# A hybrid RG-LRU and short-convolution block on one core: the first tile's root, the sums of squares of chunk 1 and the last sum arranged anew

## Chip, cores and metric

The kernel runs on one core of one Trainium2 chip. The metric is device time in microseconds (us) of one execution; lower is better. Every run is one launch of the whole block on the same inputs.

## What is computed

The block works on 1024 positions of width 1024, all in float32. The part that matters here is the first half of the layer; the last line closes the block.

```python
sc = jax.nn.silu(c)
mod = sc @ ada_w[l] + ada_b[l]
shift1, scale1, gate1, shift2, scale2, gate2 = jnp.split(mod[:, None, :], N_ADA, axis=-1)
h = rmsnorm(x, norm1_g[l]) * (1.0 + scale1) + shift1
proj = h @ w_in[l]                      # 1024 -> 2560
...
x = x + gate1 * mixed
h2 = rmsnorm(x, norm2_g[l]) * (1.0 + scale2) + shift2
x = x + gate2 * (jnp.square(jax.nn.relu(h2 @ w_mlp1[l])) @ w_mlp2[l])
...
return rmsnorm(x, final_g)
```

Between proj and mixed stand a causal convolution, an RG-LRU recurrence, a gated convolution, head-wise norms and an output projection.

## The kernel before

**Layout.** Everything is kept transposed: 128 channels on the partitions, positions along the free axis. The 1024 positions are two chunks of 512 (cc = 0 and 1), the 1024 channels eight tiles (k = 0 to 7). F[:, 8 cc + k] holds tile k of chunk cc. F[:, 16:26], E and G are scratch. A product in high precision is made of three matmuls with rounded operands (`mm3`, L105, L107, L109): each operand is split in a high half (HI, rounded) and a low half (LO, what the rounding left), kept in R; the products are low weights by high data, high by high, and high weights by low data.

**Start (L135 to L310).** SP loads the vectors (`vt`, L141), a unit matrix into G (`ident`, L172) and x of chunk 0 (four DMAs, `load_x`). TensorE spreads silu(c) over all partitions in banks 0 and 1, and VectorE copies them to `cb` (L295). ScalarE squares the eight tiles of x (L292), VectorE adds them up, and float32 matmuls with a matrix of ones (L300) put the sum of squares into bank 7. `rsq` (L119 to L124) makes the reciprocal root: ScalarE's root and its square, then two VectorE instructions that are one step of correction. 21 `warm` matmuls keep TensorE busy meanwhile (L305).

**The loop over the tiles of chunk 0 (L321 to L357).** For tile k+1 VectorE makes two columns of modulation, each with one product with a row sum over 128 x 1024 (`gemv1`, L251), of which ScalarE makes scale and shift (`mod1`, L258 and L260). `make_xn` (L238) multiplies x by the root. `make_hi` is two ScalarE passes: the high half of scale * x + shift into R (L243), and the same unrounded, in place in F (L244). `make_lo` (L247) subtracts the two on VectorE. The weights of the tile are split too: ScalarE rounds them (L327), VectorE makes the remainder (L322). Then TensorE adds the tile to seven banks: 7 blocks of `mm3`, 21 matmuls of 512 columns. The order of the loop body, without the loads:

```python
V.tensor_tensor(whl(k)[1], win1[k], fp(whl(k)[0]), op=ALU.subtract)
if k == 0:
    make_lo(0, k)
if k + 1 < KT:
    gemv1(k + 1, 0)
    A(whl(k + 1)[0], win1[k + 1], AF.Copy)
    make_xn(0, k + 1, r0)
if k:
    make_lo(0, k)
...
    gemv1(k + 1, 1)
    make_hi(0, k + 1)
```

**Sums of chunk 1.** From k = 5 on, ScalarE squares the tiles of chunk 1 (`squares1`, L315), two at a time; VectorE adds each pair and a float32 matmul adds the pair to bank 7 (`sum1`, L318 and L319): one at k = 6, three at k = 7. At k = 7 the matmuls of all banks but the first are ordered behind the last of these sums. Then `softplus2` (small VectorE instructions), `rsq`, and `make_h1` (L361 to L364) and the low half (L371) tile by tile for chunk 1.

**What sets the order.** Up to L371 VectorE, ScalarE and SP work in the order of the program (`manual_schedule`); TensorE's instructions, and everything behind, are ordered by the compiler's scheduler, with `after(a, b)` where an order is written out. ScalarE's copy of a finished bank for the gated convolution (`conv_c`, L470) belongs to what comes behind, and chunk 1's first matmuls (`chunk1`) follow it.

**End (L1043 to L1120).** The last products of the block go in quarters: for half h of chunk cc, `last_acc` adds a block to x, squares it (L1056) and scales it with final_g (L1058); `last_add` adds the square to E[:, cc]; `last_sum` sums E and the square of tile 6 with two float32 matmuls (L1065, L1066); `last_rs` is `rsq`; `last_out` multiplies with the root (L1077 to L1082) and stores (L1083).

Of the kernel before, what the change touches and what calls it, by code (L numbers as in the profile page):

```python
# [14 lines left out]
P = 128  # L15
# [20 lines left out]
def block_kernel(ctx, tc, xT, vec, adaT, winA, winB, gw, wout, w1, w2, outT):  # L36
# [5 lines left out]
    def sb(name, shape, dt=F32):  # L42
        return pool.tile(shape, dt, name=name, tag=name)
# [2 lines left out]
    R = sb("R", [P, 38, 2, H], F32R)  # L46
    F = sb("F", [P, 26, H])
    E = sb("E", [P, 4, 516])
    vt = sb("vt", [P, NV])
    sc = sb("sc", [P, KT])  # L50
    ones = sb("ones", [P, P])
    bones = sb("bones", [P, P], F32R)
# [2 lines left out]
    epsc = sb("epsc", [P, 1])  # L55
    mods = sb("mods", [P, 48])
    md = sb("md", [P, 48])
    pre = sb("pre", [P, 48])
    pg = sb("pg", [P, 8])
    lp = sb("lp", [P, 6, 4])  # L60
    gneg = sb("gneg", [P, 8])
# [10 lines left out]
    def fp(ap):  # L72
        return ap.bitcast(F32)
# [64 lines left out]
    V.memset(bf[:64, :64], 1.0)  # L138
    V.memset(bf[64:, 64:], 1.0)
    V.tensor_copy(bones, bf)  # L140
    dma(vt, vec[:, :NV])  # L141

    def f(i):
        return F[:, i, :]
# [23 lines left out]
        win1[k] = fl(r)[:, : NS * P].rearrange("p (j n) -> p j n", n=P)  # L168
        dma(win1[k], winA[k].rearrange("p (j n) -> p j n", n=P))

    ident = G[:, 0, :P]
    dma(ident, vec[:, NV:])  # L172
    for q in range(4):
        load_x(0, q)

# [86 lines left out]
    def whl(k):  # L262
        w0 = 16 + k // 4
        return R[:, w0 : w0 + 2 * NS : 2, HI, kc(k)], R[:, w0 : w0 + 2 * NS : 2, LO, kc(k)]

    ET = mybir.EngineType
    with tc.manual_schedule(engines={ET.DVE, ET.Activation, ET.SP}):
        V.tensor_scalar(neg, ap, -1.0, None, op0=ALU.mult)
        V.tensor_tensor(neg, neg, ap, op=ALU.min)
        A(e, neg, AF.Exp)  # L270

        cp = vt[:, V_C : V_C + KT]
        A(sc, cp, AF.Tanh, scale=0.5)

        A(lp[:, 5, 0:1], vt[:, 0:1], AF.Abs_reciprocal_sqrt)
        V.scalar_tensor_tensor(sc, sc, 1.0, cp, op0=ALU.add, op1=ALU.mult)
        for k in range(KT):
            i = T.matmul(banks[k // 4][:, kc(k)], lhsT=sc[:, k : k + 1].broadcast_to([P, P]), rhs=ident, start=True, stop=True)
        warm(ones, 8, i)
        V.tensor_scalar(vt[:, V_N1 : V_N1 + 24], vt[:, V_N1 : V_N1 + 24], -1.0 / (2 * D), None, op0=ALU.mult)  # L280
        V.tensor_scalar(gneg, vt[:, V_LOG : V_LOG + 8], -1.0 / 128, None, op0=ALU.mult)
        V.tensor_scalar(pre, vt[:, V_ADAB : V_ADAB + 48], 1.0, None, op0=ALU.add)
        V.tensor_tensor(pg, pre[:, 0:16:2], vt[:, V_N1 : V_N1 + 8], op=ALU.mult)
        softplus1()
        load_ada1(0)
        load_win1(0)
        load_ada1(1)
        load_win1(1)

        sq0 = [f(16), f(17), E[:, 0, :H], E[:, 1, :H], E[:, 2, :H], E[:, 3, :H], f(14), f(15)]  # L290
        for k in range(KT):
            A(sq0[k], f(k), AF.Square)  # L292
            if k % 2:
                if k < 4:
                    V.tensor_copy(cb[:, k // 2, :], banks[k // 2])  # L295
                V.tensor_tensor(sq0[k - 1], sq0[k - 1], sq0[k], op=ALU.add)
            if k == 3:
                V.tensor_tensor(sq0[0], sq0[0], sq0[2], op=ALU.add)
            if k > 2 and k % 2:
                summed = T.matmul(banks[7], lhsT=ones, rhs=sq0[0 if k == 3 else k - 1], start=k == 3, stop=k == 7)  # L300
        r0, r1 = E[:, 0, :H], E[:, 1, :H]
        for i in range(2):
            gemv1(0, i, False)
        rsq(banks[7], r0, r1, D)
        warm(ones, 21, summed)  # L305
        for i in range(2):
            mod1(0, i)
        make_xn(0, 0, r0)
        A(whl(0)[0], win1[0], AF.Copy)
        make_hi(0, 0)  # L310
        sq1 = {6: f(16), 7: f(17), 0: E[:, 1, :H], 1: E[:, 3, :H], 2: E[:, 2, :H], 3: f(17), 4: f(16), 5: E[:, 3, :H]}

        def squares1(k):
            for i in (k, k + 1):
                A(sq1[i], f(8 + i), AF.Square)  # L315

        def sum1(k):
            V.tensor_tensor(sq1[k], sq1[k], sq1[k + 1], op=ALU.add)  # L318
            return T.matmul(banks[7], lhsT=ones, rhs=sq1[k], start=k == 6, stop=k == 4)  # L319

        for k in range(KT):  # L321
            V.tensor_tensor(whl(k)[1], win1[k], fp(whl(k)[0]), op=ALU.subtract)  # L322
            if k == 0:
                make_lo(0, k)
            if k + 1 < KT:
                gemv1(k + 1, 0)
                A(whl(k + 1)[0], win1[k + 1], AF.Copy)  # L327
                make_xn(0, k + 1, r0)
            if k:
                make_lo(0, k)  # L330
            if k + 1 < KT:
                if k == 6:
                    squares1(0)
                gemv1(k + 1, 1)
                make_hi(0, k + 1)
            if k + 2 < KT:
                load_ada1(k + 2)
                load_win1(k + 2)
            if k == 4:
                load_x(1, 3)  # L340
            if k == 5:
                load_x(1, 0)
                load_x(1, 1)
                squares1(6)
            if k == 6:
# [20 lines left out]
        make_h1(0)  # L366
        for k in range(KT):
            if k + 1 < KT:
                hi_done = make_h1(k + 1)
            hi, lo = rs_(2 * k + 1)  # L370
            h_done = V.scalar_tensor_tensor(lo, f(8 + k), md[:, 2 * k + 1 : 2 * k + 2], fp(hi), op0=ALU.add, op1=ALU.subtract)  # L371


    gh, gl = sb("gh", [P, 2 * H], F32R), sb("G", [P, 2 * H], F32R)
# [676 lines left out]
    def last_acc(p, h, q):  # L1051
        cs = cols(h)
        b = ends[h][0 if p == 4 else 1 if p == 2 else 2][q][:, cs]
        cc, n = block2(p, 4 + 2 * q)
        acc2(cc, n, b, cs)
        A(f(14 + n)[:, cs], x1(cc, n)[:, cs], AF.Square)  # L1056
        if n != 6:
            A(x1(cc, n)[:, cs], x1(cc, n)[:, cs], AF.Identity, scale=vt[:, V_NF + n : V_NF + n + 1])  # L1058
# [9 lines left out]
    def last_rs(cc, h):  # L1068
        rsq(nbank[cc, h][:, :Q], E[:, cc, cols(h)], f(24)[:, cols(h)], D)

    def last_out(cc, h, first, step=4):
        cs = cols(h)
        rs = E[:, cc : cc + 1, cs]
        for n in range(0, 4, step) if first else range(4, 8, step):
            o = cc * 8 + n
            if n + step <= 6:
                V.tensor_tensor(F[:, o : o + step, cs], F[:, o : o + step, cs], rs.broadcast_to([P, step, Q]), op=ALU.mult)  # L1077
            else:
                if step == 4:
                    V.tensor_tensor(F[:, o : o + 2, cs], F[:, o : o + 2, cs], rs.broadcast_to([P, 2, Q]), op=ALU.mult)  # L1080
                V.scalar_tensor_tensor(x1(cc, 6)[:, cs], x1(cc, 6)[:, cs], vt[:, V_NF + 6 : V_NF + 7], E[:, cc, cs], op0=ALU.mult, op1=ALU.mult)
                V.tensor_tensor(x1(cc, 7)[:, cs], x1(cc, 7)[:, cs], E[:, cc, cs], op=ALU.mult)  # L1082
            dma(outT[cc, :, n : n + step, cs], F[:, o : o + step, cs])  # L1083
# [88 lines left out]
```

## Time and profile before

| what | value |
|---|---|
| device time, median of 3 runs | 980.53 us (980.26 to 981.69) |
| time of the profiled execution | 980.45 us |
| its span | 978.7 us |
| TensorE matmul (PE) busy | 963.9 us, 98%, 4448 records |
| VectorE (DVE) busy | 750.8 us, 77% |
| ScalarE (ACT) busy | 537.2 us, 55% |
| DMA, q1 | 153.77 MB, 44.8% of 16 engines' span |

The span is what the profiler saw of the core; the execution's time has 1.75 us around it. PE is the matmuls, PEld the loads of their weights, which run beside them. Ends of matmuls are modelled. Start times below count from the start of the span. In a timeline a row has start, duration, engine, line, operation, output <- inputs, sizes and the count of merged instructions; in square brackets stands how long the engine idled before it and what ended that. SPq is SP's queue of DMA issues. Buffer numbers are left out: F, E and R are the tensors named above. A column "granted clock" of 1.00 is 2.4 GHz, 0.50 is 1.2 GHz.

### The profile page before, as it was taken

To read this page: it belongs to the slowest core of one execution; us is meant where nothing else is said; L and a number is where in the kernel's file an instruction comes from. 1 tells how busy PE (TensorE), PEld (TensorE's weight loads), DVE (VectorE), ACT (ScalarE), POOL (GpSimd) and SP (SyncE) were. 2 spreads that over 40 slices of the span, in tenths; PEclk is the share of its full clock that TensorE was granted. 3 is DMA by queue.
4 is the path that set the end of the run, shared out by engine and by line. 5 is a ranking of instruction groups with operands and counts; after the bars stand their busy time and mean duration, and the time that the engine had idled before them with its cause. 6 is when DMAs were issued, how large, how long until landed. Compare 5 with 4: busy or idle time off the path is not lost.

```text
span 978.7 us, 11651 instructions
## 1 busy us (share of the span) xinstructions
PE 963.9 (98%) x4448; PEld 800.2 (82%) x4448; DVE 750.8 (77%) x1001; ACT 537.2 (55%) x719; POOL 0.2 (0%) x4
## 2 busy tenths in 40 slices
PE   8999999999999999999999999999999999999996
PEld 7878787788888998888888888887888888888885
DVE  7989999976545799785655555798598599589757
ACT  6778888885412677555464554683253243144444
POOL 0000000000000000000000000000000000000000
PEclk9999999999999999999999999999999999999998
DMA  8925236234222131774443524789356157144005
GB/s 313 344 100 183 89 138 210 74 125 172 78 95 97 50 115 63 258 255 175 172 145 124 204 104 177 264 286 357 124 173 215 65 172 236 65 151 172 1 1 172
DMA packets 53288, 154.52 MB, mean 158 GB/s; under 512 B 5104, under 2 KB 10736, under 8 KB 53232
## 3 DMA queue, kind: packets, MB, share of 16 engines
q1 hardware_dynamic: 53232, 153.77, 44.8%
q8 instruction: 35, 0.57, 0.2%
q14 instruction: 21, 0.17, 0.0%
HBM read 116.00 MB, written 37.75 MB: 157 GB/s over the span
## 4 chain that ended last, share of the span: by engine, by line
PE 84%; DVE 10%; ACT 3%; DMA 2%; issue 1%; SPq 0%; DVEq 0%; ACTq 0%
PE bank L105 28%; PE bank L109 27%; PE bank L107 27%; DVE R L101 2%; DVE F L212 1%; DVE F L434 1%; DVE F L465 1%; DMA E<-hidd 1%; ACT F L407 1%; DMA gh<-hidd 0%; DMA F<-xT 0%; ACT R L100 0%; DVE F L463 0%; DVE F L466 0%; DMA hidd<-E 0%
## 5 line engine op out<-in xcount | busy, mean ns | idle before, releaser
L105 PE MATMUL bank<-R 128*128 128x512 f32 (+1 forms) x1416 | 522.3, 380 | 1.3 <-ACT R L364 0.6
L107 PE MATMUL bank<-R 128*128 128x512 f32 (+1 forms) x1416 | 519.8, 379 | 0.0
L109 PE MATMUL bank<-R 128*128 128x512 f32 (+1 forms) x1416 | 516.7, 379 | 0.0
L105 PEld LDWEIGHTS bank<-R 128*128 128x128 f32 x1416 | 266.3, 188 | 54.5 <-DVE F L996 1.9
L109 PEld LDWEIGHTS bank<-R 128*128 128x128 f32 x1416 | 266.1, 188 | 50.6 <-DVE R L247 0.4
L107 PEld LDWEIGHTS bank<-R 128*128 128x128 f32 x1416 | 266.4, 188 | 50.3 <-issue 0.7
L100 ACT ACTIVATE R<-F 128x1024 fp32r<-128x1024 f32 (+1 forms) x175 | 165.6, 958 | 175.8 <-PE bank L109 117.6
L101 DVE TENSOR_TENSOR R<-F,R 128x1024 fp32r<-128x1024 f32 (+1 forms) x175 | 189.4, 1098 | 58.0 <-ACT R L100 57.8
L996 DVE SCALAR_TENSOR_TENSOR F<-bank,md,F 128x512 f32<-128x512 f32 (+1 forms) x120 | 84.9, 712 | 49.0 <-PE bank L109 47.7
L909 ACT ACTIVATE F<-bank 128x512 f32<-128x512 f32 x44 | 26.2, 597 | 48.8 <-PE bank L109 48.3
L100 ACT ACTIVATE R<-G 128x1024 fp32r<-128x1024 f32 x23 | 24.3, 1057 | 32.8 <-PE bank L109 22.0
L101 DVE TENSOR_TENSOR R<-G,R 128x1024 fp32r<-128x1024 f32 x23 | 28.1, 1221 | 13.0 <-ACT R L100 13.0
L100 ACT ACTIVATE R<-E 128x1024 fp32r<-128x1024 f32 x26 | 27.4, 1052 | 10.1 <-DMA E<-hidd 10.0
L101 DVE TENSOR_TENSOR R<-E,R 128x1024 fp32r<-128x1024 f32 x26 | 31.7, 1218 | 0.1
L212 DVE SCALAR_TENSOR_TENSOR F<-F 128x1024 f32<-128x1024 f32 x24 | 29.1, 1217 | 1.3 <-DMA F<-adaT 1.3
L585 ACT ACTIVATE E<-F 128x512 f32<-128x512 f32 (+1 forms) x21 | 11.1, 527 | 32.3 <-DVE F L583 30.3
L407 ACT ACT_TABLE_LOAD x22 | 28.2, 1283 | 0.4
L909 ACT ACTIVATE E<-bank 128x512 f32<-128x512 f32 x20 | 11.9, 595 | 23.4 <-PE bank L109 23.4
L583 DVE SCALAR_TENSOR_TENSOR F<-bank,md,F 128x512 f32<-128x512 f32 (+1 forms) x21 | 12.7, 620 | 15.6 <-PE bank L109 15.6
L924 ACT ACTIVATE F<-bank 128x512 f32<-128x512 f32 x16 | 9.5, 597 | 19.9 <-PE bank L109 18.5
L913 ACT ACTIVATE F<-F 128x1024 f32<-128x1024 f32 x18 | 18.9, 1049 | 2.6 <-DVE F L943 1.5
L914 ACT ACTIVATE F<-F 128x1024 f32<-128x1024 f32 x18 | 19.0, 1058 | 0.4
(198 smaller groups left out, 738.2 us busy)
## 6 DMA issues: line engine op xcount, KB each, us to landing
F<-w SPq DMA_DIRECT2D x51, 512.0 KB, 4.2
hidd<-F SPq DMA_DIRECT2D x47, 512.0 KB, 4.5
F<-adaT SPq DMA_DIRECT2D x44, 512.0 KB, 4.1
E<-hidd SPq DMA_DIRECT2D x26, 512.0 KB, 5.7
F<-xT SPq DMA_DIRECT2D x16, 512.0 KB, 5.8
F<-hidd SPq DMA_DIRECT2D x15, 512.0 KB, 4.4
gh<-hidd SPq DMA_DIRECT2D x15, 512.0 KB, 4.9
F<-winB SPq DMA_DIRECT2D x13, 512.0 KB, 3.2
```

What stands on the lines that cost most here:

```text
L100: a = A(dst[0], src, AF.Copy)
L101: return a, V.tensor_tensor(dst[1], src, fp(dst[0]), op=ALU.subtract)
L105: i = [T.matmul(b, lhsT=wl, rhs=xh, start=start, stop=False, **kw) for b, xh, xl in outs]
L107: T.matmul(b, lhsT=wh, rhs=xh, start=False, stop=False, **kw)
L109: T.matmul(b, lhsT=wh, rhs=xl, start=False, stop=stop, **kw)
L212: g = V.scalar_tensor_tensor(fl(r), fl(r), 0.5, fl(cb) if cv is None else cv, op0=ALU.mult, op1=ALU.mult, accum_out=mods[:, idx : idx + 1])
L407: i = A(*args, **kw)
L583: V.scalar_tensor_tensor(x, b, gate(16, n), x, op0=ALU.mult, op1=ALU.add)
L909: A(t[:, q, :], bk2[q], AF.Copy)
L913: A(t, t, AF.Relu)
L914: A(t, t, AF.Square)
L996: done_by["bank"] = V.scalar_tensor_tensor(x1(cc, n)[:, cs], b, gate(40, n), x1(cc, n)[:, cs], op0=ALU.mult, op1=ALU.add)
```

## The change

All vectors and the unit matrix come with one load into a longer `vt`; `ident` and `pre` are views of it, and the +1 is made in place. Of the first eight squares the last is made by VectorE, and the copy of bank 1 by ScalarE. For the first tile of each chunk the correction of the root is no longer finished ahead of the scaling: `first_h` multiplies the tile by column and uncorrected root, then by the corrected factor, and `full_root` finishes the root for the other tiles afterwards. Tiles 0 and 7 of chunk 0 get their low half by `shift_lo`; tiles 1 to 6 get `make_lo` at another place of the loop body. Two squares of chunk 1 are made by VectorE, and its eight squares are summed with three float32 matmuls, all at k = 7. At the end, the last quarter's squares are summed with three matmuls, without the last VectorE add, and the last tiles are scaled in pairs.

```diff
-    vt = sb("vt", [P, NV])
+    vt = sb("vt", [P, NV + P])
-    pre = sb("pre", [P, 48])
-    dma(vt, vec[:, :NV])
+    dma(vt, vec)
-    ident = G[:, 0, :P]
-    dma(ident, vec[:, NV:])
+    ident = vt[:, NV:]
+    pre = vt[:, V_ADAB : V_ADAB + 48]
...
+    def first_h(x, g, r0, r1):
+        V.scalar_tensor_tensor(x, x, g, r0, op0=ALU.mult, op1=ALU.mult)
+        V.scalar_tensor_tensor(r1, banks[7], D * EPS, r1, op0=ALU.add, op1=ALU.mult)
+        V.scalar_tensor_tensor(x, r1, -3.0 * D, x, op0=ALU.add, op1=ALU.mult)
+    def full_root(r0, r1):
+        V.scalar_tensor_tensor(r0, r1, -3.0 * D, r0, op0=ALU.add, op1=ALU.mult)
+    def shift_lo(cc, k):
+        hi, lo = rs_(2 * k + cc)
+        return V.scalar_tensor_tensor(lo, f(cc * 8 + k), md[:, 2 * k + 1 : 2 * k + 2], fp(hi), op0=ALU.add, op1=ALU.subtract)
...
-        V.tensor_scalar(pre, vt[:, V_ADAB : V_ADAB + 48], 1.0, None, op0=ALU.add)
+        for i in (0, 24):
+            V.tensor_scalar(pre[:, i : i + 16 : 2], pre[:, i : i + 16 : 2], 1.0, None, op0=ALU.add)
...
+        V.tensor_copy(cb[:, 0, :], banks[0])
         for k in range(KT):
-            A(sq0[k], f(k), AF.Square)
+            if k + 1 < KT:
+                A(sq0[k], f(k), AF.Square)
+                if k == 5:
+                    A(cb[:, 1, :], banks[1], AF.Copy)
+            else:
+                V.tensor_tensor(sq0[k], f(k), f(k), op=ALU.mult)
             if k % 2:
-                if k < 4:
-                    V.tensor_copy(cb[:, k // 2, :], banks[k // 2])
...
-        rsq(banks[7], r0, r1, D)
         warm(ones, 21, summed)
-        for i in range(2):
-            mod1(0, i)
-        make_xn(0, 0, r0)
+        A(r0, banks[7], AF.Abs_reciprocal_sqrt, bias=epsc, scale=1.0 / D)
+        mod1(0, 0)
+        A(r1, r0, AF.Square)
+        mod1(0, 1)
         A(whl(0)[0], win1[0], AF.Copy)
-        make_hi(0, 0)
+        first_h(f(0), md[:, 0:1], r0, r1)
+        A(rs_(0)[0], f(0), AF.Identity, bias=md[:, 1:2])
...
         def squares1(k):
             for i in (k, k + 1):
-                A(sq1[i], f(8 + i), AF.Square)
+                if k == 2:
+                    V.tensor_tensor(sq1[i], f(8 + i), f(8 + i), op=ALU.mult)
+                else:
+                    A(sq1[i], f(8 + i), AF.Square)
...
         for k in range(KT):
             V.tensor_tensor(whl(k)[1], win1[k], fp(whl(k)[0]), op=ALU.subtract)
             if k == 0:
+                shift_lo(0, 0)
+                full_root(r0, r1)
+            if k == 7:
+                squares1(2)
+                shift_lo(0, 7)
+            elif k:
                 make_lo(0, k)
             if k + 1 < KT:
                 gemv1(k + 1, 0)
                 A(whl(k + 1)[0], win1[k + 1], AF.Copy)
-                make_xn(0, k + 1, r0)
-            if k:
-                make_lo(0, k)
-            if k + 1 < KT:
-                if k == 6:
-                    squares1(0)
+                if k < 6:
+                    make_xn(0, k + 1, r0)
+                else:
+                    V.scalar_tensor_tensor(f(7), f(7), md[:, 14:15], r0, op0=ALU.mult, op1=ALU.mult)
                 gemv1(k + 1, 1)
-                make_hi(0, k + 1)
+                if k < 6:
+                    make_hi(0, k + 1)
+                else:
+                    A(rs_(14)[0], f(7), AF.Identity, bias=md[:, 15:16])
...
             if k == 6:
                 last = load_x(1, 2)
-                sum1(6)
-                squares1(2)
+                add1(6, 7)
+                squares1(0)
             if k == 7:
-                sum1(0)
                 squares1(4)
+                add1(0, 1)
+                add1(0, 6)
+                sum1(0, start=True)
+                add1(2, 3)
                 sum1(2)
-                summed = sum1(4)
+                add1(4, 5)
+                summed = sum1(4, stop=True)
                 softplus2()
...
-        rsq(banks[7], f(16), f(17), D)
+        q0, q1 = f(16), f(17)
+        A(q0, banks[7], AF.Abs_reciprocal_sqrt, bias=epsc, scale=1.0 / D)
+        A(q1, q0, AF.Square)
+        first_h(f(8), md[:, 0:1], q0, q1)
+        A(rs_(1)[0], f(8), AF.Identity, bias=md[:, 1:2])
+        full_root(q0, q1)
...
-                last_add(cc, h, 4)
+                if (cc, h) != (1, 1):
+                    last_add(cc, h, 4)
                 done.append((cc, h))
-        last_sum(*done[-1])
+        b, cs = nbank[1, 1][:, :Q], cols(1)
+        for i, t in enumerate((E[:, 1, cs], f(18)[:, cs], f(20)[:, cs])):
+            T.matmul(b, lhsT=ones, rhs=t, start=i == 0, stop=i == 2)
+        last_scale(1, 1, 4)
         last_out(*done[-2], False)
         last_rs(*done[-1])
-        last_out(*done[-1], True, 2)
-        last_out(*done[-1], False, 2)
+        last_scale(1, 1, 6)
+        for n in range(0, KT, 2):
+            o = KT + n
+            V.tensor_tensor(F[:, o : o + 2, cs], F[:, o : o + 2, cs], E[:, 1:2, cs].broadcast_to([P, 2, Q]), op=ALU.mult)
+            dma(outT[1, :, n : n + 2, cs], F[:, o : o + 2, cs])
```

The squares of tiles 4 and 5 of chunk 1 are kept in G instead of F and E; `add1` is the VectorE add and `sum1` the matmul of the old `sum1`, taken apart. `last_scale` is the scaling of `last_acc` (L1058), which the last quarter's tiles 4 and 6 get after the sum.

## Rows read from the trace of the kernel before

**Rows 1.** The page's part 4: the chain that ended last, by engine.

```profile
PE 84%; DVE 10%; ACT 3%; DMA 2%; issue 1%; SPq 0%; DVEq 0%; ACTq 0%
```

**Rows 2.** Stretches: us, busy of PE, PEld, DVE, ACT, POOL (count), granted clock, DMA share, GB/s.

```profile
23.30:60.30 37.00, 37.00 (x155) 28.92 (x155) 34.18 (x67) 26.72 (x44) 0.00 (x0) 1.00 0.80 289
60.30:670.00 609.70, 606.88 (x2777) 503.79 (x2777) 457.88 (x613) 377.21 (x508) 0.00 (x0) 1.00 0.43 153
...
970.80:973.00 2.20, 0.00 (x0) 0.00 (x0) 1.29 (x4) 0.86 (x2) 0.00 (x0) 0.84 0.53 178
```

**Rows 3.** Timeline of DVE, tiles 1 and 2 of chunk 0 (start, us).

```profile
21.96 1.08 DVE L322 TENSOR_TENSOR R<-F,R 128x896 fp32r<-128x896 f32 x1
22.97 1.22 DVE L251 SCALAR_TENSOR_TENSOR F<-F 128x1024 f32<-128x1024 f32 x1
...
24.72 0.68 DVE L247 TENSOR_TENSOR R<-F,R 128x512 fp32r<-128x512 f32 x1
...
26.46 1.08 DVE L322 TENSOR_TENSOR R<-F,R 128x896 fp32r<-128x896 f32 x1
```

**Rows 4.** Timeline of ACT beside them.

```profile
26.57 0.29 ACT L260 ACTIVATE md<-mods,vt 128x1 f32<-128x1 f32 x1 [1.12 <-DVE F L251]
26.90 0.81 ACT L243 ACTIVATE R<-F,md 128x512 fp32r<-128x512 f32 x1
27.75 0.82 ACT L244 ACTIVATE F<-F,md 128x512 f32<-128x512 f32 x1
```

**Rows 5.** Timeline of DVE: the low half of the first and the last tile.

```profile
18.46 0.69 DVE L247 TENSOR_TENSOR R<-F,R 128x512 fp32r<-128x512 f32 x1 [0.79 <-ACT F L244]
...
51.69 0.69 DVE L247 TENSOR_TENSOR R<-F,R 128x512 fp32r<-128x512 f32 x1 [1.04 <-ACT F L244]
```

**Rows 6.** Timeline of SP's DMA queue at the start.

```profile
1.18 0.42 SPq L172 DMA_DIRECT2D G<-vec  x1
...
1.65 1.85 SPq L147 DMA_DIRECT2D F<-xT  x4
```

**Rows 7.** Timeline of all engines at the start.

```profile
11.23 0.69 DVE L296 TENSOR_TENSOR F<-F 128x512 f32<-128x512 f32 x1 [0.49 <-ACT F L292]
...
12.94 4.85 PE L201 MATMUL bank<-ones 128*128 128x128 f32 x42
...
13.14 0.69 ACT L121 ACTIVATE E<-bank,epsc 128x512 f32<-128x512 f32 x1 [1.94 <-PE bank L300]
...
14.39 0.37 ACT L258 ACTIVATE md<-mods,pg,vt 128x1 f32<-128x1 f32 x1
...
15.97 0.69 DVE L238 TENSOR_TENSOR F<-F,E 128x512 f32<-128x512 f32 x1
...
17.78 0.19 PEld L105 LDWEIGHTS bank<-R 128*128 128x128 f32 x1 [0.19 <-ACT R L243]
```

**Rows 8.** Timeline of DVE and ACT, last tile of chunk 0 to chunk 1.

```profile
48.96 0.07 DVE L251 DVE_READ_ACCUMULATOR F<-F 128x1 f32 x1
...
56.40 0.69 ACT L121 ACTIVATE F<-bank,epsc 128x512 f32<-128x512 f32 x1 [1.31 <-PE bank L319]
...
59.84 0.60 ACT L470 ACTIVATE F<-bank 128x512 f32<-128x512 f32 x1 [2.09 <-PE bank L109]
```

**Rows 9.** The chain of waits in the same place (start, us, what).

```profile
53.78 2.58 PE bank L319 x6
...
61.10 0.50 PE bank L105
```

**Rows 10.** Timeline of ACT, PE and DVE at the end.

```profile
969.37 0.40 ACT L1056 ACTIVATE F<-F 128x256 f32<-128x256 f32 x1
969.60 0.70 PE L1065 MATMUL bank<-E,ones 128*128 128x256 f32 x2 [0.91 <-DVE E L1061]
970.14 0.59 PE L1066 MATMUL bank<-F,ones 128*128 128x256 f32 x2
974.85 0.42 DVE L1082 TENSOR_TENSOR F<-F,E 128x256 f32<-128x256 f32 x1
```

More of the change, by code (lines that the diff above doesn't have):

```diff
@@ L303, in block_kernel, with add1, sum1 @@
             gemv1(0, i, False)
-        rsq(banks[7], r0, r1, D)
         warm(ones, 21, summed)
-        for i in range(2):
-            mod1(0, i)
-        make_xn(0, 0, r0)
+        A(r0, banks[7], AF.Abs_reciprocal_sqrt, bias=epsc, scale=1.0 / D)
+        mod1(0, 0)
+        A(r1, r0, AF.Square)
+        mod1(0, 1)
         A(whl(0)[0], win1[0], AF.Copy)
-        make_hi(0, 0)
-        sq1 = {6: f(16), 7: f(17), 0: E[:, 1, :H], 1: E[:, 3, :H], 2: E[:, 2, :H], 3: f(17), 4: f(16), 5: E[:, 3, :H]}
+        first_h(f(0), md[:, 0:1], r0, r1)
+        A(rs_(0)[0], f(0), AF.Identity, bias=md[:, 1:2])
+        sq1 = {6: f(16), 7: f(17), 0: E[:, 1, :H], 1: E[:, 3, :H], 2: E[:, 2, :H], 3: f(17), 4: G[:, 0, :], 5: G[:, 1, :]}
         def squares1(k):
             for i in (k, k + 1):
-                A(sq1[i], f(8 + i), AF.Square)
-        def sum1(k):
-            V.tensor_tensor(sq1[k], sq1[k], sq1[k + 1], op=ALU.add)
-            return T.matmul(banks[7], lhsT=ones, rhs=sq1[k], start=k == 6, stop=k == 4)
+                if k == 2:
+                    V.tensor_tensor(sq1[i], f(8 + i), f(8 + i), op=ALU.mult)
+                else:
+                    A(sq1[i], f(8 + i), AF.Square)
+        def add1(k, i):
+            V.tensor_tensor(sq1[k], sq1[k], sq1[i], op=ALU.add)
+        def sum1(k, start=False, stop=False):
+            return T.matmul(banks[7], lhsT=ones, rhs=sq1[k], start=start, stop=stop)
         for k in range(KT):
@@ L364, in make_h1 @@
             return A(R[:, 2 * k + 1, HI, :], xk, AF.Identity, bias=sh)
-        make_h1(0)
         for k in range(KT):
@@ L369, in block_kernel @@
                 hi_done = make_h1(k + 1)
-            hi, lo = rs_(2 * k + 1)
-            h_done = V.scalar_tensor_tensor(lo, f(8 + k), md[:, 2 * k + 1 : 2 * k + 2], fp(hi), op0=ALU.add, op1=ALU.subtract)
+            h_done = shift_lo(1, k)
     gh, gl = sb("gh", [P, 2 * H], F32R), sb("G", [P, 2 * H], F32R)
@@ L1056, in last_acc, with last_scale @@
         A(f(14 + n)[:, cs], x1(cc, n)[:, cs], AF.Square)
-        if n != 6:
-            A(x1(cc, n)[:, cs], x1(cc, n)[:, cs], AF.Identity, scale=vt[:, V_NF + n : V_NF + n + 1])
+        if n != 6 and not (n == 4 and (cc, h) == (1, 1)):
+            last_scale(cc, h, n)
+    def last_scale(cc, h, n):
+        x = x1(cc, n)[:, cols(h)]
+        A(x, x, AF.Identity, scale=vt[:, V_NF + n : V_NF + n + 1])
     def last_add(cc, h, n):
@@ L1069, in last_rs, with last_out @@
         rsq(nbank[cc, h][:, :Q], E[:, cc, cols(h)], f(24)[:, cols(h)], D)
-    def last_out(cc, h, first, step=4):
+    def last_out(cc, h, first):
         cs = cols(h)
         rs = E[:, cc : cc + 1, cs]
[L1074 to L1083, printed above, removed]
+        n = 0 if first else 4
+        o = cc * 8 + n
+        if first:
+            V.tensor_tensor(F[:, o : o + 4, cs], F[:, o : o + 4, cs], rs.broadcast_to([P, 4, Q]), op=ALU.mult)
+        else:
+            V.tensor_tensor(F[:, o : o + 2, cs], F[:, o : o + 2, cs], rs.broadcast_to([P, 2, Q]), op=ALU.mult)
+            V.scalar_tensor_tensor(x1(cc, 6)[:, cs], x1(cc, 6)[:, cs], vt[:, V_NF + 6 : V_NF + 7], E[:, cc, cs], op0=ALU.mult, op1=ALU.mult)
+            V.tensor_tensor(x1(cc, 7)[:, cs], x1(cc, 7)[:, cs], E[:, cc, cs], op=ALU.mult)
+        dma(outT[cc, :, n : n + 4, cs], F[:, o : o + 4, cs])
     with tc.manual_schedule(engines={ET.DVE, ET.Activation, ET.PE}):
```

## The prediction

> **What bounds the kernel now.** I read the chain that ended last first: 84% of it is TensorE [rows 1]. Then the stretches [rows 2]: from 23.3 to 60.3 us TensorE is busy 37.00 of 37.00, and from 60.3 to 670 it idles 609.70 - 606.88 = 2.8 us in all. So what reaches the end is only what delays or frees TensorE: its first matmul, the eight tiles of chunk 0, the step to chunk 1 at 61.10 [rows 9], and the tail after its last matmul. The 155 matmul records of 23.3 to 60.3 are 147 of the projection and 8 of the four float32 sums; six of the latter take 2.58 us [rows 9], 0.43 each, so one projection matmul takes (37.00 - 8 x 0.43) / 147 = 0.228 us and one tile (21 of them) 4.79 us. That is TensorE's beat.
>
> Next, VectorE's beat beside it: it begins the weight remainder (L322) of tile 1 at 21.96 and of tile 2 at 26.46 [rows 3], so 4.50 us a tile with no gap. VectorE is ahead of TensorE by only 0.29 us a tile. Tile k's matmuls need its high half from ScalarE, and ScalarE gets its scale and shift from the two column products (L251) of that tile, so VectorE's beat is also the beat at which tiles are released.
>
> **Part 1, the place of the low half: the costly part.** The diff's words are of roots and sums, but in the loop `make_lo(0, k)` of tiles 1 to 6 is moved too: from behind the next tile's first product and `make_xn` to right behind the weight remainder. It subtracts the high half from the tile that ScalarE's second pass (L244) leaves. When can it start? With tile 2: its second column product ends when the remainder starts, 26.46 [rows 3]; then ScalarE makes the shift at 26.57, the high half at 26.90, the second pass at 27.75, which ends at 27.75 + 0.82 = 28.57 [rows 4], 2.11 us after the products. VectorE has only the remainder to do meanwhile, 22.97 - 21.96 = 1.01 us [rows 3]. So it stands 1.1 us. The kernel before shows that wait at just the two tiles where the low half already follows the remainder: 0.79 at tile 0 and 1.04 at tile 7, both for L244 [rows 5]. At tile 1 (24.72, [rows 3]) there is none, because a product and `make_xn` stand before it.
>
> Everything on VectorE behind the low half waits with it: both products of the next tile, hence the shift, hence the high half that TensorE wants. The beat becomes 4.50 + 1.1 = 5.6 us, over TensorE's 4.79: VectorE becomes the bound of this stage, and the lead of 0.29 doesn't matter any more. From the products of tile 1 to those of tile 6 that is 5 x 1.1 = **+5.5 us**. From tile 6 to 7 it is 1.1 again, and the new `scalar_tensor_tensor` on f(7) takes the modulation column itself, so it waits for ScalarE's column (0.37 us, [rows 7], and about 0.11 of delay as from 26.46 to 26.57): 0.5 more, **+1.6 us**. Not hidden: TensorE is out of work at each tile.
>
> **Part 2, the start.** One load of vectors takes one issue from SP: the x loads, issued at 1.65 behind the second vec load at 1.18 [rows 6], go 0.47 earlier. The first sum of squares ends on VectorE's add at 11.23 [rows 7], which follows the last x. Bounds: 0.47 earlier if x lands by its issue, nothing if the bytes set it; I take 0.4, since the bytes ahead are the same and the issue is what moves. The copy of banks[1] that goes to ScalarE and the square that goes to VectorE change places at equal length (0.6 to 0.7 us each); the +1 in place is one more small instruction, in a wait for TensorE; both at nothing, covered by the wait for x (0.2 at most otherwise). The matrix now in vt frees G, so the loads of tile 1 are issued earlier; nobody waits for them.
>
> Merged root: before, ScalarE's root starts at 13.14 and the scaled tile on VectorE at 15.97 [rows 7], 2.83 us for root, square and two half steps. After, root (0.7), column (0.4), product with column and root (0.7) and one half (0.7) lie in a row, and the square and the other half beside them: 2.5, so 0.3 less. Then the wait of 0.79 [rows 5] before tile 0's low half goes (the high half is ready in time), against 0.6 of the full root now placed there: 0.2 less. The products of tile 1 end 0.4 + 0.3 + 0.2 = **-0.9 us**. TensorE's first matmul can't use all of that: the 21 warm matmuls (42 records, 4.85 us from 12.94, so to 17.79) fill its queue until the first weights load at 17.78 [rows 7], and they move only with the first sum. But tile 1's release, and with it all that follows, goes by VectorE.
>
> **Part 3, from tile 7 to chunk 1.** Before: products of tile 7 end at 48.96 [rows 8], chunk 1 starts at 61.10 [rows 9]: 12.1 us. After, counted from that end, VectorE does add 0.6, remainder 1.0, two squares 1.2, low half 0.7, two adds 1.4 (512 columns cost 0.6 to 0.7 each, as the 0.68 of [rows 3]), so the first sum can start at 4.9 (before, one of the four sums was already done by then and the rest were hidden behind tile 6's matmuls). Three sums of 0.86 end at 7.5; 18 matmuls that are ordered behind them take 4.1: TensorE is done at 11.6. Beside it the merged root: 0.7, then VectorE's `softplus2` for 0.5 more, three steps 2.1, ScalarE 0.7: also 11.6. But ScalarE's copy of the conv bank (L470) stood ahead of the high half and waited 2.09 for TensorE [rows 8]; if it stays there, 12.4. I take 12.2: **+0.1**. So the sum that is saved (0.86) and the shorter root don't show, because the sums come later.
>
> **Part 4, the clock.** Around tile 7 TensorE now has about 0.7 us of work in 5 us (end of tile 6 until the first sum). In the tail, four matmuls from 969.60 to 970.73 [rows 10] and nothing else, the granted clock is 0.84 in 970.80 to 973.00 [rows 2], that is, it fell to 1.2 GHz late in that stretch. So it may fall here. Bounds: nothing, or three sums and 18 matmuls at half speed, 2.58 + 4.1 = 6.7. I take **+1.0**, near the lower end, because in the tail it fell late in the stretch, and at tile 7 the work is about to return by then. The Trainium skill, "TensorE: Matmul & The Clock Gate", section "HAM oscillation — how this bites in real kernels", tells that long gaps between matmuls put the array back to the lower clock; by that rule the sum would lie between 986.3 and 993, and the tail's 0.84 agrees with it.
>
> **Part 5, the end.** The add at 969.13 and its way into the first sum matmul (969.60, waiting 0.91 for VectorE) go; the last sum matmul then waits for the square of 969.37, which ends at 969.77, instead of starting at 970.14 [rows 10]: -0.3. The last scaling is one instruction of about 0.68 in place of two ending at 974.85 + 0.42: -0.15. Together **-0.5** (nothing if the last stores set the end).
>
> **Sum.** -0.9 + 5.5 + 1.6 + 0.1 + 1.0 - 0.5 = +6.8 us. The profiled execution took 980.45 (span 978.7), 0.1 below the median of 980.53: 980.45 + 6.8 = **987.3 us**. What can be got back later is at most the 2.8 us that TensorE idles up to 670.
>
> **Rivals.** *Faster, 977.6.* If the low half did not hold VectorE, TensorE would stay the bound: 0.9 from the start, 0.9 for one sum, 0.6 from the root (the matmuls of chunk 0 end at 53.78 + 2.58 + 18 x 0.228 = 60.5, and chunk 1 starts at 61.10 [rows 9]), 0.5 at the end: -2.9. For it: each piece is real, and TensorE is busy 37.00 of 37.00. Against it: the two waits of [rows 5]. It decides only if VectorE's beat stays under 4.79, that is with a wait below 0.29 a tile; I get 1.1. Chance 0.09. *The clock stays low, 993.* Place: the gap at tile 7; price 6.7 in place of 1.0; for it the tail's 0.84, against it that in the stretches where TensorE works with short gaps the granted clock is 1.00 [rows 2]. Chance 0.07. *No change.* The delay would have to be taken up almost whole; the 2.8 us of idle don't hold it. Chance 0.03. The forecast keeps 0.81.
>
> **Range.** Low: no clock term and all 2.8 us got back, 987.3 - 3.8 = 983.5. High: half of the 6.7 (2.4 more) and no gain at the start (0.9): 990.5. A measurement here tells about 0.2% (2.0 us): faster 0.09, same 0.03, slower 0.07 + 0.81 = 0.88.
>
> **What would show it.** Right: waits of about 1.1 us before the low halves of tiles 1 to 6, all for L244's successor; TensorE idle about 0.8 us ahead of tiles 2 to 7; chunk 1 starting near 67 us instead of 61.10; three sums (6 records) together at tile 7 after a gap; a span from the last matmul to the end shorter by 0.5. Wrong: TensorE without gaps between tiles 2 and 6; or chunk 1 starting near 59 us; or, if chunk 1 starts near 67 and the total doesn't follow, a stage behind it that waited for something else.

## The result and the profile after

The change makes the kernel **slower by 0.91%**: 989.8 us (median of 4 runs, 989.29 to 992.02) against 980.7 us, a ratio of 1.0091 (95% interval 1.0077 to 1.0104). The forecast was 987.3 us with a range of 983.5 to 990.5, so direction and range held and the time lies 2.5 us above the forecast. The profiled execution took 989.89 us, its span 988.0, so 9.3 us more than the span before (978.7).

The page's chain by engine, of after: VectorE's share is larger, TensorE's smaller than in [rows 1].

```profile
PE 79%; DVE 12%; ACT 4%; DMA 2%; issue 2%; DVEq 0%; SPq 0%
```

Where that happens is seen in stretches of after (columns as in [rows 2]: the stretch, its length, busy time of PE, PEld, DVE, ACT, POOL with counts, then granted clock, DMA share, GB/s).

```profile
23.00:55.40 32.40, 29.62 (x124) 22.37 (x123) 26.59 (x42) 18.09 (x30) 0.00 (x0) 1.00 0.80 283
55.40:59.00 3.60, 0.85 (x3) 0.30 (x3) 3.60 (x8) 3.10 (x6) 0.00 (x0) 1.00 0.77 267
59.00:60.00 1.00, 0.57 (x1) 0.18 (x1) 0.98 (x3) 0.39 (x1) 0.00 (x0) 0.65 0.87 332
60.00:66.00 6.00, 5.67 (x7) 2.53 (x8) 3.27 (x18) 1.01 (x3) 0.00 (x0) 0.50 0.02 10
66.00:67.00 1.00, 1.00 (x5) 0.79 (x4) 0.42 (x1) 0.97 (x2) 0.00 (x0) 0.94 0.00 0
70.00:680.00 610.00, 607.83 (x2780) 503.98 (x2779) 457.94 (x613) 375.53 (x507) 0.00 (x0) 1.00 0.44 153
```

Before, TensorE was busy without a gap from 23.3 us to the end of chunk 0 [rows 2]. Now it idles 2.8 us between 23.0 and 55.4 and 2.75 us of the 3.6 behind that, and then works for 6 us at a granted clock of 0.50, that is 1.2 GHz in place of 2.4. From 70 us on it idles as little as before.

VectorE's timeline of after, the counterpart of [rows 3, 5] (start, us, line, operation, and in brackets the idle time before it and who ended that):

```profile
20.95 1.08 DVE L346 TENSOR_TENSOR R<-F,R 128x896 fp32r<-128x896 f32 x1
23.09 0.69 DVE L246 TENSOR_TENSOR R<-F,R 128x512 fp32r<-128x512 f32 x1 [1.05 <-ACT F L243]
...
26.59 1.09 DVE L346 TENSOR_TENSOR R<-F,R 128x896 fp32r<-128x896 f32 x1
28.73 0.69 DVE L246 TENSOR_TENSOR R<-F,R 128x512 fp32r<-128x512 f32 x1 [1.05 <-ACT F L243]
...
53.58 0.75 DVE L361 SCALAR_TENSOR_TENSOR F<-F,md,E 128x512 f32<-128x512 f32 x1 [0.46 <-ACT md L257]
...
55.39 0.08 DVE L250 DVE_READ_ACCUMULATOR F<-F 128x1 f32 x1
```

The remainder (L346) of tile 1 and that of tile 2 are now 26.59 - 20.95 = 5.64 us apart, where [rows 3] had 4.50, and in front of each low half (L246) VectorE stands 1.05 us for ScalarE's second pass (L243). The pattern repeats for all six tiles. Tile 7 adds the 0.46 us for ScalarE's column (L257), so its products end at 55.39 in place of 48.96 [rows 8].

What TensorE waited for between 23 and 60 us, of after (the line that waited, what for: us in total, times, longest):

```profile
PE bank L104 <- ACT R L242: 2.8, 5, 0.6
PE bank L104 <- DVE R L346: 1.7, 1, 1.7
PE bank L108 <- DVE R L276: 1.1, 1, 1.1
```

The five waits of 0.55 us stand ahead of tiles 2 to 6, each for that tile's high half (L242), which VectorE's late products have delayed. TensorE's timeline at the last of them (ahead of tile 6) and around tile 7:

```profile
49.52 0.39 PE L108 MATMUL bank<-R 128*128 128x512 f32 x1
50.46 0.50 PE L104 MATMUL bank<-R 128*128 128x512 f32 x1 [0.55 <-ACT R L242]
50.80 0.39 PE L106 MATMUL bank<-R 128*128 128x512 f32 x1
...
57.23 0.47 PE L104 MATMUL bank<-R 128*128 128x512 f32 x1 [1.67 <-DVE R L346]
57.53 0.40 PE L106 MATMUL bank<-R 128*128 128x512 f32 x1
59.00 0.57 PE L108 MATMUL bank<-R 128*128 128x512 f32 x1 [1.07 <-DVE R L276]
60.33 3.78 PE L343 MATMUL bank<-E,ones 128*128 128x512 f32 x4 [0.76 <-DVE E L340]
63.91 1.92 PE L343 MATMUL bank<-G,ones 128*128 128x512 f32 x2
...
69.96 0.39 PE L104 MATMUL bank<-R 128*128 128x512 f32 x1
```

Between 55.6 and 60.3 us TensorE has three matmuls and three gaps. The clock falls there, and the three sums (6 records), whose slots in the chain of waits sum to the next row, take 5.49 us. In [rows 9] six records took 2.58, with no wait in front of them.

```profile
60.33 5.49 PE bank L343 x6
```

Chunk 1 starts at 69.96 instead of 61.10 [rows 9]: 8.86 us later, of the 9.3 in all.

At the start (timeline of after, against [rows 7]) the root and the first weights come earlier, but the warm matmuls still hold TensorE's first work:

```profile
12.60 4.85 PE L200 MATMUL bank<-ones 128*128 128x128 f32 x42
...
12.80 0.69 ACT L322 ACTIVATE E<-bank,epsc 128x512 f32<-128x512 f32 x1 [2.25 <-PE bank L317]
...
17.20 0.48 PE L104 MATMUL bank<-R 128*128 128x512 f32 x1
```

And at the end (timeline of after, against [rows 10]) the root follows the last projection matmul by 980.02 - 977.98 = 2.04 us, before by 2.35:

```profile
977.98 0.28 PE L108 MATMUL bank<-R 128*128 128x256 f32 x1
...
980.02 0.47 ACT L120 ACTIVATE E<-bank,epsc 128x256 f32<-128x256 f32 x1 [0.39 <-PE bank L1155]
...
981.89 2.50 DVE L1162 TENSOR_TENSOR F<-F,E 128x512 f32<-128x512 f32 x4
```

### The profile page after: what moved, and what is told of

Its sections match the earlier page's. It is cut to its first block, busy times and chain, and to the rows that moved or that the text cites. A ratio compares the mean times of both kernels' runs of the same rounds, so it can differ in the third digit from the quotient of the medians.

```text
span 988.0 us, 11650 instructions
## 1 busy us (share of the span) xinstructions
PE 969.3 (98%) x4448; PEld 801.1 (81%) x4448; DVE 753.5 (76%) x1005; ACT 533.9 (54%) x716; POOL 0.2 (0%) x4
## 4 chain that ended last, share of the span: by engine, by line
PE 79%; DVE 12%; ACT 4%; DMA 2%; issue 2%; DVEq 0%; SPq 0%
PE bank L104 26%; PE bank L106 26%; PE bank L108 26%; DVE R L100 2%; DVE F L211 1%; DVE F L250 1%; DVE F L503 1%; ACT F L445 1%; DMA hidd<-F 1%; PE bank L343 1%; DVE F L472 1%; DMA F<-xT 1%; DMA gh<-hidd 1%; ACT F L243 1%; ACT R L242 0%
```

## The experiments

My theory after this reading: the place of the low half in tiles 1 to 6 costs about 6 us, the fall of the clock at tile 7 about 3, and the rest of the change roughly cancels. The rivals: the late sums and the merged root of chunk 1 cost the time and the low half is hidden; or the clock is a bystander, and the gap at tile 7 would cost as much without it. Eight kernels tell them apart. The kernel before, run beside them, had medians of 981.17 us (17 runs, beside the first four) and 981.09 us (27 runs, beside the other four). The ratios are taken over all runs and differ a little from the quotients of the medians. The start of chunk 1 is that of one execution each.

| kernel | median us (runs) | ratio to before, 95% | chunk 1 starts |
|---|---|---|---|
| after | 989.8 (4) | 1.0091 (1.0077 to 1.0104) | 69.96 |
| after, low halves back | 983.46 (8) | 1.0019 (1.0005 to 1.0033) | 62.67 |
| before, low halves moved | 986.58 (4) | 1.0058 (1.0043 to 1.0073) | 67.21 |
| after, filled gap | 987.01 (4) | 1.0063 (1.0048 to 1.0078) | 66.89 |
| before, new start | 980.55 (10) | 0.9996 (0.9986 to 1.0005) | 60.12 |
| before, new end | 981.34 (1) | one run | 61.60 |
| after, low halves back, filled gap | 981.5 (11) | 1.0002 (0.9993 to 1.0011) | 61.96 |
| new start, root and end, sums early | 979.7 (11) | 0.9989 (0.998 to 0.9997) | 59.15 |
| the same with the four sums of before | 979.91 (11) | 0.9988 (0.9979 to 0.9997) | 59.64 |

**The low halves back.** The change, with one thing undone:

```diff
-            elif k:
-                make_lo(0, k)
             if k + 1 < KT:
...
                     V.scalar_tensor_tensor(f(7), f(7), md[:, 14:15], r0, op0=ALU.mult, op1=ALU.mult)
+                if k:
+                    make_lo(0, k)
                 gemv1(k + 1, 1)
```

> The changed kernel, with the low halves of tiles 1 to 6 back behind the next tile's scaling; everything else of the change stays. Theory 1 (the place of the low half costs the time): VectorE's beat is 4.50 us a tile again in place of 5.64, TensorE has no gap between tiles 2 and 6, the products of tile 7 end near 49.4 us in place of 55.39. The three sums still come after VectorE's work at tile 7, 4.9 us later (54.3), so chunk 1 starts near 61 us and the total is 980.2 us (979 to 983), about the kernel before. Theory 2 (the merged roots or the three late sums cost it): the total stays above 986. Theory 3 (without the low half the change is a gain in full): 977.6.

Measured: 983.46 us, so 6.3 us under the kernel after, and 3.3 us over what I expected. VectorE's beat is 4.50 us again, TensorE has no gap at tiles 2 to 6, and tile 7's products end at 49.26. What I hadn't foreseen is left at tile 7 (TensorE's timeline of this kernel, then its stretches):

```profile
52.88 0.50 PE L108 MATMUL bank<-R 128*128 128x512 f32 x1 [1.07 <-DVE R L276]
54.20 3.29 PE L343 MATMUL bank<-E,ones 128*128 128x512 f32 x4 [0.83 <-DVE E L340]
57.29 1.45 PE L343 MATMUL bank<-G,ones 128*128 128x512 f32 x2
```

```profile
54.00:55.00 1.00, 0.80 (x2) 0.49 (x3) 1.00 (x3) 0.68 (x2) 0.00 (x0) 0.87 1.04 360
55.00:58.00 3.00, 3.00 (x4) 1.09 (x4) 1.57 (x12) 0.00 (x0) 0.00 (x0) 0.50 0.22 89
58.00:59.00 1.00, 1.00 (x4) 0.57 (x3) 0.57 (x5) 0.22 (x1) 0.00 (x0) 0.93 0.00 0
```

The clock falls here too, with two gaps of about a microsecond only. So the fall doesn't need the moved low halves: sums that come late are enough. It may not fall in every run: of the 8, 5 had a mean granted clock of 0.995 to 0.996 (983.28 to 985.24 us) and 3 one of 0.998 to 0.999 (980.54 to 982.77 us). Only the profiled run (0.995) shows where; the mean alone is no proof, since two of the 27 runs of the kernel before stand at 0.996 too.

**Only the low halves moved.** The kernel before, with one thing changed:

```diff
-            if k == 0:
-                make_lo(0, k)
+            make_lo(0, k)
             if k + 1 < KT:
...
                 make_xn(0, k + 1, r0)
-            if k:
-                make_lo(0, k)
```

> The kernel before, with nothing changed but the place of the low halves of tiles 1 to 6 (right behind the weight remainder). Theory 1: VectorE stands 1.05 us before each, the beat is 5.64 us, the products of tile 7 end near 55.8 us in place of 48.96, chunk 1 starts near 66.6 in place of 61.10, the total is 986.0 us (985 to 987.5) without a fall of the clock, since one sum stands behind tile 6 and the gap before the others is short. Theory 2: at most 982.

Measured: 986.58 us, 5.4 us over the kernel before, and a span of 984.8, 6.1 over its. This one move makes over half of the loss. VectorE's timeline and the stretch around tile 7 of this kernel:

```profile
24.03 0.69 DVE L247 TENSOR_TENSOR R<-F,R 128x512 fp32r<-128x512 f32 x1 [1.06 <-ACT F L244]
```

```profile
50.00:70.00 20.00, 17.95 (x66) 11.68 (x65) 16.76 (x41) 14.76 (x25) 0.00 (x0) 1.00 0.49 177
```

The wait is the same 1.06 us, but the clock stays at 1.00: the first of the four sums still runs at 56.47, ahead of tile 7's matmuls, and no gap behind it is longer than 0.77 us. Chunk 1 starts at 67.21, 6.11 us late, and all of it arrives at the end of the span.

**The gap filled.** The kernel after, with 14 matmuls on the matrix of ones put behind tile 6; they write into the bank of the sums, which the first sum overwrites, so this is extra work and nothing is left out:

```diff
+NFILL = 14
...
             if k == 7:
+                for _ in range(NFILL):
+                    w = T.matmul(banks[7][:, :P], lhsT=ones, rhs=ones, start=True, stop=True)
+                    after(w, tile6)
                 squares1(4)
...
+                if k == 6:
+                    tile6 = i
```

> The changed kernel with 14 matmuls of ones of 128 columns behind tile 6's matmuls, into the sums' bank before the sums begin, in the gap in which TensorE idles; their result is overwritten. If the fall of the clock at tile 7 costs what the sums show (5.49 us in place of 2.58), the granted clock is 1.00 throughout, the three sums take 2.6 us, chunk 1 starts near 66.9 us in place of 69.96, and the total is 986.7 us (986 to 987.5). If the sums are slow for another reason (their operands, a wait), they stay at 5.5 us and the total is 989.8.

Measured: 987.01 us, 2.8 us under the kernel after, with more work in it. TensorE's timeline (each matmul of ones has two records), the chain of waits at the sums, and the stretch of this kernel:

```profile
55.16 3.29 PE L383 MATMUL bank<-ones 128*128 128x128 f32 x28
...
60.11 1.98 PE L344 MATMUL bank<-E,ones 128*128 128x512 f32 x4 [0.83 <-DVE E L341]
61.93 1.02 PE L344 MATMUL bank<-G,ones 128*128 128x512 f32 x2
...
66.89 0.39 PE L105 MATMUL bank<-R 128*128 128x512 f32 x1
```

```profile
60.11 2.84 PE bank L344 x6
```

```profile
50.00:70.00 20.00, 18.93 (x89) 14.49 (x90) 17.73 (x42) 11.76 (x21) 0.00 (x0) 1.00 0.42 157
```

The sums start as late as without the fill (60.11 against 60.33), but run at the full clock, in 2.84 us of the chain in place of 5.49. Chunk 1 follows tile 7's products (55.17 here) by 11.7 us in place of 14.57. The clock is a cause, and its price here is 2.8 us. With the 5.4 us of the moved low halves that is 8.2 of the 8.6 us between the medians of after (989.8) and of the kernel before beside these runs (981.17).

**The start alone.** The kernel before with the new start: one load of vectors, a square on VectorE, the root merged with tile 0.

```diff
-    dma(vt, vec[:, :NV])
+    dma(vt, vec)
...
-        rsq(banks[7], r0, r1, D)
         warm(ones, 21, summed)
-        for i in range(2):
-            mod1(0, i)
-        make_xn(0, 0, r0)
+        A(r0, banks[7], AF.Abs_reciprocal_sqrt, bias=epsc, scale=1.0 / D)
+        mod1(0, 0)
+        A(r1, r0, AF.Square)
+        mod1(0, 1)
         A(whl(0)[0], win1[0], AF.Copy)
-        make_hi(0, 0)
+        first_h(f(0), md[:, 0:1], r0, r1)
+        A(rs_(0)[0], f(0), AF.Identity, bias=md[:, 1:2])
...
-                make_lo(0, k)
+                shift_lo(0, 0)
+                full_root(r0, r1)
```

> The kernel before with the start of the change alone: one load of vectors, the columns' +1 in place, bank 1 copied by ScalarE, the last square by VectorE, the merged root of chunk 0, tile 0's low half by one instruction. Theory 1: the first matmul of the projection at 17.2 us in place of 17.78 (held by the warm matmuls), tile 1's products end at 20.95 in place of 21.96, TensorE stays the bound, chunk 1 starts near 60.1 in place of 61.10, the total is 979.5 us (979 to 980.2). Rival (the start is hidden by what follows): 980.5.

Measured: 980.55 us, a ratio of 0.9996 with an interval around 1. The step itself works: tile 1's products end at 20.94, and chunk 1 starts 0.98 us earlier, at 60.12. The time doesn't decide between the two forecasts: the interval of 0.9986 to 1.0005 holds the whole gain of 1.0 us (0.999) and none. The one trace shows the lead shrink: at the first head-norm sum it is 0.9, at the last 0.5. Most of that goes at one sum (TensorE's timeline, before and this kernel):

```profile
183.88 0.50 PE L416 MATMUL bank<-R,bones 128*128 128x512 f32 x1 [0.72 <-DVE F L123]
```

```profile
183.40 0.50 PE L436 MATMUL bank<-R,bones 128*128 128x512 f32 x1 [1.05 <-DVE F L122]
```

TensorE waits there for VectorE's step of the root, 1.05 us in place of 0.72, and VectorE, which works without a gap from 164.70 us up to that step, comes to it only 0.48 earlier (182.67 against 183.15). The rest goes by 690 us, but it can't be laid to the start: TensorE's busy time from 632 to 690 us, in the kernel before, in this one and in the kernel with the new end alone, which has the code of before in this stretch, is

```profile
632.00:690.00 58.00, 57.49 (x253) 46.78 (x252) 50.62 (x50) 33.22 (x37) 0.00 (x0) 1.00 0.91 318
632.00:690.00 58.00, 57.12 (x250) 46.36 (x249) 50.78 (x50) 32.62 (x36) 0.00 (x0) 1.00 0.90 315
632.00:690.00 58.00, 56.83 (x249) 46.31 (x248) 49.85 (x50) 33.80 (x37) 0.00 (x0) 1.00 0.92 318
```

so the idle time is 0.51, 0.88 and 1.17 us, and executions of the same code differ by 0.66. The chain that ended last goes through transfers here: a store of 6.79 us in this kernel (hidd<-F at 667.54), one of 6.24 with the new end alone (at 668.44).

**The end alone.** The kernel before with the new end, cut to its core:

```diff
-                last_add(cc, h, 4)
+                if (cc, h) != (1, 1):
+                    last_add(cc, h, 4)
...
-        last_sum(*done[-1])
+        b, cs = nbank[1, 1][:, :Q], cols(1)
+        for i, t in enumerate((E[:, 1, cs], f(18)[:, cs], f(20)[:, cs])):
+            T.matmul(b, lhsT=ones, rhs=t, start=i == 0, stop=i == 2)
```

> The kernel before with the end of the change alone. From the last matmul of a product to the end of the span: 10.0 us in place of 10.3, of which the sum brings 0.3 and the scaling 0.1, and the last store gives back 0.2. The time itself can't show that.

Measured: the root starts 2.05 us after the last projection matmul (969.60 to 971.65), and the span ends 10.0 us after it, in place of 10.3: a gain of 0.3 us. The time of this one run (981.34 us) lies within the runs of the kernel before and tells nothing by itself.

**Low halves back, gap filled.** The first experiment with 10 of the third one's matmuls:

```diff
+NFILL = 10
...
             if k == 7:
+                for _ in range(NFILL):
+                    w = T.matmul(banks[7][:, :P], lhsT=ones, rhs=ones, start=True, stop=True)
+                    after(w, tile6)
...
```

> The changed kernel with the low halves at the old place and 10 matmuls of ones behind tile 6's, whose result is overwritten. If what the kernel with the old place alone still loses (983.5 in place of 980.2 expected) is the clock that falls in most of its runs, the clock is 1.00 throughout, the three sums take 2.6 us, and the total is 980.7 us (980 to 981.5) with a spread of 2 us or less. If it is something else: 983.

Measured: 981.5 us, a ratio of 1.0002. So what the first experiment still lost was the clock in the main: 983.46 - 981.5 = 2.0 us by the medians; in the two traces chunk 1 follows the first sum by 6.8 us (55.19 to 61.96) in place of 8.5 (54.20 to 62.67), which is 1.7. The granted clock is 1.00 in this kernel's stretch below. All other parts of the change together are worth nothing that can be measured.

```profile
50.00:70.00 20.00, 19.89 (x92) 15.21 (x91) 19.25 (x44) 11.29 (x18) 0.00 (x0) 1.00 0.24 84
```

**What is good in the change, without its waits.** The new start, merged root and end; the low halves at their old place; all squares on ScalarE; and the three sums fed by adds that stand on VectorE ahead of tile 7's low half:

```diff
             V.tensor_tensor(whl(k)[1], win1[k], fp(whl(k)[0]), op=ALU.subtract)
+            if k == 7:
+                add1(0, 1)
+                add1(0, 6)
...
-                if k == 2:
-                    V.tensor_tensor(sq1[i], f(8 + i), f(8 + i), op=ALU.mult)
-                else:
-                    A(sq1[i], f(8 + i), AF.Square)
+                A(sq1[i], f(8 + i), AF.Square)
...
```

> A version meant to beat both: the start of the change, the merged root of chunk 1, three sums and the last sum in parts, but the low halves at the old place, tile 7 made as before, all squares of chunk 1 on ScalarE, and the adds of the first sum put into VectorE's wait ahead of tile 7's low half, so that the sums start without a long gap of TensorE. Theory 1 (place of the low half, and late sums that let TensorE idle and its clock fall, are all that is wrong with the change): sums end near 54.5 us at full clock, chunk 1 starts near 59 us in place of 61.10, the end is 0.3 shorter: 978.5 us by the profile of before (977.8 to 979.8). Rival (a gain at the start is lost behind, as it was with the start alone, where 1.0 us at chunk 1 left 0.1 in the profile): 980 or more.

Measured: 979.7 us, a ratio of 0.9989 (0.998 to 0.9997), under the kernel before but by less than I expected. Chunk 1 starts at 59.15, 1.95 us earlier. The next kernel and the one with the new start alone split this: 0.98 for the start (60.12), 0.48 for the merged root of chunk 1 (59.64; the wait of 0.62 us for ScalarE in front of chunk 1 is gone), 0.49 for the sum that is saved (counted from the warm matmuls, whose start varies, 0.63, 0.80 and 0.78). The sums no longer wait behind a gap (TensorE's timeline of this kernel):

```profile
52.11 1.02 PE L340 MATMUL bank<-E,ones 128*128 128x512 f32 x2
...
53.20 1.02 PE L340 MATMUL bank<-E,ones 128*128 128x512 f32 x2
...
54.10 1.12 PE L340 MATMUL bank<-G,ones 128*128 128x512 f32 x2
```

From 632 to 690 us TensorE idles 1.30 us (before 0.51), in two waits for VectorE's scaled tiles (L1026). The chain that ended last goes there through a load of the block's x of 7.63 us (F<-x1d at 667.34). As the kernel with the new end alone idles 1.17 us in this stretch with the code of before, this can't be laid to the change either. Where the rest of the lead goes stays open.

**The same with four sums.** In place of the three sums, the four of before (the edit is against the last kernel):

```diff
-            if k == 7:
-                add1(0, 1)
-                add1(0, 6)
...
-                add1(6, 7)
+                sum1(6)
                 squares1(2)
             if k == 7:
+                sum1(0)
                 squares1(4)
-                sum1(0, start=True)
-                add1(2, 3)
                 sum1(2)
-                add1(4, 5)
-                summed = sum1(4, stop=True)
+                summed = sum1(4)
...
```

> As the version with three sums, but with the four sums of the kernel before (one behind tile 6). Chunk 1 starts near 59.4 to 60 us, the root merged but one sum more (0.86 us of TensorE): 979.2 us (978.5 to 980.3). Rival as there: 980 or more.

Measured: 979.91 us, a ratio of 0.9988 (0.9979 to 0.9997). Chunk 1 starts 0.49 us later than with three sums (0.78 later counted from the warm matmuls, which began 0.29 apart), which is what one sum saves net, and none of that shows in the time (979.91 against 979.7, with overlapping intervals). Both versions are under the kernel before, by about 0.1%, which is under the 0.2% that the prediction set as what tells a change from none; they beat it by the edge of an interval, no more.

## Why the prediction was right, and where it was off

The terms of the sum against the spans of the two profiled executions:

| step | taken | measured |
|---|---|---|
| start, to the end of tile 1's products | -0.9 | 20.95 - 21.96 = -1.0 |
| five tiles | +5.5 | 5 x (5.64 - 4.50) = +5.7 |
| tile 6 to 7 | +1.6 | 6.24 - 4.50 = +1.7 |
| tile 7 to chunk 1, without the clock (gap filled) | +0.1 | 11.72 - 12.14 = -0.4 |
| clock at tile 7 | +1.0 | 14.57 - 11.72 = +2.9 |
| chunk 1 to the last matmul | 0 | 9.56 - 8.86 = +0.7 |
| end | -0.5 | 10.02 - 10.28 = -0.26 |
| sum | +6.8 | +9.3 |

**Part 1 held**, and it carries the result. In the timelines of the loop VectorE works in the order of the program, the low half stands in front of the next tile's products, and the wait is the 1.05 us that [rows 5] let one read. The kernel with this move alone showed it: +6.1 us in the span. The profile's gaps on TensorE are 0.55 us a tile, not the 0.8 foreseen, but the loss is 0.8: the matmuls on the two sides of a gap start 0.94 us apart (49.52 and 50.46), where others start 0.23 apart, and the next one follows after 0.34. The profile counts a matmul as busy for 0.39 us, longer than the distance to the next start, so its gap looks shorter. The beat is VectorE's either way.

**Part 2 came out within 0.1 us, in part by luck.** Counted from the warm matmuls, tile 1's products end after 8.35 us in place of 9.02 (12.60 to 20.95, before 12.94 to 21.96): the merged root brings 0.7, where 0.5 was foreseen. The other 0.3, taken as 0.4 for the earlier x loads, can't be told from chance: in seven kernels with the same new start the warm matmuls began anywhere from 12.37 to 13.52. That these matmuls keep TensorE's first work from moving as far was right. The prediction saw that up to 2.8 us of idle can *give back* a delay, not that a lead can shrink as well, as the trace of the start alone shows.

**Part 3** had two ends, 11.6 and 12.4 us from tile 7's products to chunk 1, by whether ScalarE's copy of the conv bank stands ahead of the high half. I took the middle; the high half (68.70) went ahead of the copy (69.48), and with the gap filled, so without the fall of the clock, the stretch took 11.7 us (55.17 to 66.89): the lower end was right, and the middle was 0.5 too long. The sums started 4.94 us after the products, 4.9 foreseen.

**Part 4 is the step that failed in size.** I took 1.0 of bounds 0 to 6.7, "near the lower end, because in the tail it fell late in the stretch, and at tile 7 the work is about to return by then". The fall was late indeed, at 0.65 in 59 to 60 us, but the work that returned did not bring the clock back at once: the sums run from 60.33, and the clock is still 0.50 up to 66 us. At the full clock six records behind a wait take 2.84 us (gap filled). So the sums cost 5.49 - 2.84 = 2.65 us more and the matmul behind them 0.2: 2.9 in all. With the gap filled the time fell by 2.8. The rule that the prediction set beside this term (the Trainium skill, "TensorE: Matmul & The Clock Gate", section "HAM oscillation — how this bites in real kernels": long gaps between matmuls put the array back to the lower clock) pointed the right way, though the page speaks of long gaps and here no single one was longer than 1.67 us; the 986.3 to 993 worked out by it hold the result. The term's own error, 1.9 us, makes most of the 2.5 by which the forecast was short.

**Part 5** was right in its first half: the root came 0.31 earlier for 0.3 foreseen. The last scaling gained 0.13, but the span ended 3.6 us after it in place of 3.4, so the last stores gave that back.

**The rivals.** The faster one fell as priced: it needed a wait below 0.29 us a tile, and 1.05 came. With the low half at its old place and the clock kept, the change came out at 1.0002: the loss is gone, so its point of decision was the right one, but of the 2.9 us it promised nothing was measured. There the sums still come late; with the sums early as well, 1.1 us came (0.9989). Of "the clock stays low, 993" less than half of the price came true, 2.9 of 6.7 us.

**What stays open:** how much of a lead of 1 to 2 us at chunk 1 is kept up to the end; the traces show where it shrinks in one execution each, and no run isolates it. The 0.7 us between chunk 1 and the last matmul of after (908.0 us in place of 907.3) need no cause in the change: with the new end alone, whose code is that of before up to the last quarter, this stretch took 908.0 us too (61.60 to 969.60).

## What to carry to other kernels

Before an instruction is moved forward on an engine that works in the order of the program, find when its latest operand is ready and add what is queued behind it: a wait already in the trace at the same kind of place prices the move, times the passes of the loop. When reductions are merged to save matmuls, look at what they filled: here one sum less brought 0.5 to 0.8 us at chunk 1 where the sums were placed early, and where all sums came after a gap, the clock cost 2.8 us. A gain ahead of a stage that waits for other things must be followed to the end of the span before it is counted, and set against what two executions of the same code differ by there.

## What the runs showed of the hardware

- TensorE's clock fell to 1.2 GHz without any single long gap: in the kernel after, the longest was 1.67 us, in a stretch of 4.8 us with three matmuls; with the low halves back, gaps of 1.07 and 0.83 us around one matmul were followed by a fall. In the kernel after the clock then stayed low from about 59.3 to 66.1 us (0.65 in 59 to 60, 0.50 in 60 to 66, 0.94 in 66 to 67), though the work was nearly without gaps from 60.33 on.
- Work that computes nothing can pay: 14 matmuls of ones in the gap (3.29 us) made the kernel 2.8 us faster than without them.
- The start varies between kernels with the same start: the warm matmuls behind the first sum began at 12.37 to 13.52 us in the seven kernels with the new start, and at 12.86 to 13.46 in the three with the old. That is more than a microsecond between single executions, and from 632 to 690 us TensorE's idle time differed by 0.66 us between two executions of the same code. So 0.1% (1 us) is not to be read from one run each.
